# A weight stream through 51 pages: raw weights held by a table, or by the pages left free

## The chip, the cores and the metric

The kernel runs on one core of one Trainium2 chip. The core has a matrix engine (TensorE: PE in the profile, its weight loads PEld), a vector engine (VectorE: DVE), a scalar engine (ScalarE: ACT), a general engine (GpSimd: POOL) and a queue engine that issues transfers (SyncE: SP). Each takes its instructions in the order of the program and waits at semaphores for the others. The metric is the device time of one execution in microseconds (us); lower is better.

## The reference, cut to what matters

One layer of an encoder for 256 positions of width 2048, in float32: a gated feed-forward block, a mixer with two attention branches, a second feed-forward block, and an embedding gate; a layer norm follows each of the first three.

```
def _layer(x):                       # SEQ 256, D_MODEL 2048, D_FF 5632, DEPTH 1
    x = _layer_norm(ALPHA * x + 0.5 * _swiglu(x, ffn1_w1, ffn1_w3, ffn1_w2), ln1_g, ln1_b)
    mix = _hybrid_mixer(x, w_in, b_gates_m, conv_m, norm_m, w_up_m, w_up_sb, w_out)
    x = _layer_norm(ALPHA * x + mix, ln2_g, ln2_b)
    x = _layer_norm(ALPHA * x + 0.5 * _swiglu(x, ffn2_w1, ffn2_w3, ffn2_w2), ln3_g, ln3_b)
    return x + jax.nn.sigmoid(x @ w_ple_gate) * (p @ w_ple_proj)

def _swiglu(x, w1, w3, w2):
    return (jax.nn.silu(x @ w1) * (x @ w3)) @ w2

def _hybrid_mixer(...):
    mq, mk, mv, mo, mi, mf, sq, sk, sv, ga, gb = _split_cols(x @ w_in)
    ...                              # mLSTM heads -> y_m, stick-breaking heads -> y_sb
    merged = jax.nn.sigmoid(ga) * (y_m @ w_up_m) + jax.nn.sigmoid(gb) * (y_sb @ w_up_sb)
    return merged @ w_out
```

## The kernel before, in words

Nearly all the time goes into products of activations with weights that are read once from memory. A **raw** weight is a tile of 256 rows by 512 columns (512 KB). PE takes float32 as two halves of a narrower type (fp32r), so each weight is **split**: ACT casts the raw tile to the high half (line 1275), DVE subtracts that from the raw tile for the low half (line 1279). A **unit** is one weight times one block of 128 positions: six matmuls of 512 columns, three for each 128 rows: high by high (line 1331), high by low (1332), low by high (1333). The first matmul reads the high half of the weight and the second one the low half. The program has 1532 units and 1088 split weights.

Most weights are read by two units, one for each block of positions. In large parts of the feed-forward blocks and of the mixer a Strassen-like scheme (`seven`) stands in for eight products: it makes seven weights out of four raw tiles by adding raw tiles to each other, and each of them is read by one unit alone. Some of these sums are made by DVE (line 371, `plus`), some by a transfer that adds into the raw tile (line 377, `plus_load`, issued from POOL's queue right behind the subtraction of the weight before it, `soon`). `weave` puts the units of such a group between those of plain groups.

Raw tiles, split halves, and the activations all live in one pool of 51 **pages** of 4 KB per partition. A page that is given up goes to the next tile that is asked for; whoever writes that tile first waits until the last reader of the old one is done. A raw tile takes one page, a split weight two.

The order of all instructions is written out by a planner as the program is built. After every unit it lets due tasks run (evictions of results, transposes, the steps of the attention heads), then calls `splits_due` (line 1290), which splits weights while fewer than a limit are held; every split calls `loads`, which issues raw loads on SP's queue while fewer than a limit are held. Both limits come from `limits(j)` and the table

```
HELD = {"ffn": (11, 6), "mix": (6, 6), "woven": (9, 6), "wide": (11, 6)}
```

as (raw, split) for the stretch of the program that weight `j` is in; within six weights of a border between blocks they are 4 and 11. "ffn" holds for both feed-forward blocks, "woven" and then "wide" for the part of the mixer in which a second product is woven into the first, "mix" for the rest.

Of the kernel before, what the change touches and what calls it, by code (L numbers as in the profile page):

```python
# [24 lines left out]

PAGES = 51
TEMP_BUFS = 6


HELD = {"ffn": (11, 6), "mix": (6, 6), "woven": (9, 6), "wide": (11, 6)}  # L30
RAW_EDGE, SPLIT_EDGE = 4, 11
EDGE = 6

# [1 line left out]
PSUM_BUFS = 8  # L35
# [149 lines left out]
    return [p[0] for p in pairs] + [p[1] for p in pairs]  # L185


@with_exitstack
def kernel(
    ctx: ExitStack,  # L190
    tc: tile.TileContext,
    x, p, ffn1_w1, ffn1_w3, ffn1_w2, ln1_g, ln1_b, w_in, b_gates_m, conv_m, norm_m,
    w_up_m, w_up_sb, w_out, ln2_g, ln2_b, ffn2_w1, ffn2_w3, ffn2_w2, ln3_g, ln3_b,
    w_ple_gate, w_ple_proj, out,
):
    nc = tc.nc
    x, out = x[0], out[0]
    p = p[0, 0]
    w_in, w_out, w_up_m, w_up_sb = w_in[0], w_out[0], w_up_m[0], w_up_sb[0]

    consts = ctx.enter_context(tc.tile_pool(name="consts", bufs=1))
    dram_pool = ctx.enter_context(tc.tile_pool(name="dram", bufs=1, space=bass.MemoryType.DRAM))
    page_pool = ctx.enter_context(tc.tile_pool(name="page", bufs=PAGES))
    temp_pool = ctx.enter_context(tc.tile_pool(name="temp", bufs=TEMP_BUFS))
    small = ctx.enter_context(tc.tile_pool(name="small", bufs=4))
    ps_pool = ctx.enter_context(tc.tile_pool(name="ps", bufs=PSUM_BUFS, space=bass.MemoryType.PSUM))
    ctx.enter_context(tc.manual_schedule())

    sched = Sched()
    temps = [0]  # L210
# [49 lines left out]
    def load_x(c, t):  # L260
        nc.sync.dma_start(out=xres(t, c * COL), in_=x[t * P:(t + 1) * P, c * COL:(c + 1) * COL])
# [1004 lines left out]
    def split_one():  # L1266
        j = pos["split"]
        w = weights[j]
        make(j)
        assert w.made or not w.make  # L1270
        r = w.raw.tile[:, :, :w.cols]
        splits[j] = [page_pool.tile([P, 2, COL], F32R, name="split", tag="page") for _ in range(2)]
        hi, lo = (h[:, :, :w.cols] for h in splits[j])
        for ks in pieces(j):
            nc.scalar.copy(hi[:, ks], r[:, ks])  # L1275
# [3 lines left out]
            nc.vector.tensor_tensor(out=lo[:, ks], in0=r[:, ks], in1=hi[:, ks], op=ALU.subtract)  # L1279
        pos["split"] += 1  # L1280
        for f in w.soon:
            assert f.raw.tile is not None
            f.make()
            f.made = True
        pos["raw"] -= len(w.frees)
        for r in w.frees:
            r.tile = None
        loads()

    def splits_due():  # L1290
        most = pos["at"] + 3 if pos["at"] < 8 else len(weights)
        while pos["split"] < most and len(splits) < limits(pos["split"])[1]:
            split_one()
            if at_edge(pos["split"]):
                break

    for c in range(4):
        if c == 0:
            load_x(0, 0)
            loads(1)  # L1300
        for t in range(TT):
            if c:
                load_x(c, t)
            sched.spawn(start(c, t), max(0.01 * t, 5.2 * c + 1.3 * t - 2.6))
        loads(2 * c + 2)
    sched.run()
    split_one()
    sched.now = 0.02
    sched.run()
    splits_due()  # L1310
    warm(WARM2)
    make_tri()
    for u in program:
        if isinstance(u, (Boundary, Mode)):
            continue
# [12 lines left out]
        for k in range(2):  # L1328
            hi, lo = a[:, 0, u.sub + k], a[:, 1, u.sub + k]
            first, last = u.start and k == 0, u.stop and k == 1  # L1330
            nc.tensor.matmul(ps, hi, w[0][:, k, :u.cols], start=first, stop=False, skip_group_check=u.onto)  # L1331
            nc.tensor.matmul(ps, hi, w[1][:, k, :u.cols], start=False, stop=False, skip_group_check=u.onto)  # L1332
            nc.tensor.matmul(ps, lo, w[0][:, k, :u.cols], start=False, stop=last, skip_group_check=u.onto)  # L1333
# [35 lines left out]
```

## Time and profile before

| | |
|---|---|
| median of 3 runs | 2166.02 us (2165.04 to 2168.65) |
| the profiled execution | 2164.03 us |
| its span, first to last instruction | 2162.3 us |
| mean granted TensorE clock | 1.000 |
| instructions | 27685 |
| bytes moved | 535.98 MB, mean 248 GB/s |

The profile is of one execution. Its page gives, for each engine, the busy time and its share of the span; then the chain of work that ended last; then groups of equal instructions with count, total and mean; and, for each group, how long its engine stood idle just before it and what ended that. Matmuls are pipelined: one takes 0.39 us from start to end, but the next one starts after 0.23 us, so that busy times of matmuls overlap. Other views answer for one window of time, one source line or one engine's waits. Times within the execution are counted from the span's start.

### The profile page before, as it was taken

What the parts mean: (1) busy time and instruction counts of PE and PEld (TensorE: products, weight loads), DVE (VectorE), ACT (ScalarE), POOL (GpSimd) and SP (SyncE); (2) the same over time, 40 slices, a digit from 0 to 9 for tenths busy, and PEclk for the clock granted to TensorE, in tenths of its full rate; (3) what the DMA queues carried; (4) which work ended last, traced back from release to release, by engine and by line L of the source; (5) the groups of instructions that cost most, each with busy time, mean ns of one, the idle gap of its engine ahead of it and who ended that gap; (6) DMA issues with size and microseconds to landing.
All of it is one profiled execution on the core that took longest, in us unless ns stands there. A gap on an engine that the chain in (4) does not pass through costs nothing.

```text
span 2162.3 us, 27685 instructions
## 1 busy us (share of the span) xinstructions
PE 2153.1 (100%) x9798; PEld 1782.0 (82%) x9798; DVE 1897.6 (88%) x2096; ACT 1344.6 (62%) x1663; POOL 218.2 (10%) x186
## 2 busy tenths in 40 slices
PE   9999999999999999999999999999999999999999
PEld 7888888888888888888888888888888888888887
DVE  6899999999998898887888975799999999999974
ACT  7656656666665765677866563556656656666572
POOL 0111111111000000101011000011111111110000
PEclk9999999999999999999999999999999999999999
DMA  9899899999994667978898976579989999999642
GB/s 350 220 272 271 248 269 277 273 277 269 266 316 148 211 217 217 244 212 208 263 276 264 274 259 206 200 191 277 267 245 279 277 272 270 265 273 301 233 168 86
DMA packets 283179, 535.98 MB, mean 248 GB/s; under 512 B 17144, under 2 KB 34464, under 8 KB 283040
## 3 DMA queue, kind: packets, MB, share of 16 engines
q1 hardware_dynamic: 234624, 440.87, 60.0%
q0 software_dynamic: 48416, 93.33, 24.0%
q8 instruction: 77, 1.26, 0.2%
q14 instruction: 62, 0.51, 0.1%
HBM read 527.85 MB, written 6.29 MB: 247 GB/s over the span
## 4 chain that ended last, share of the span: by engine, by line
PE 91%; DVE 4%; issue 3%; DMA 2%; ACT 0%; POOL 0%; SPq 0%; DVEq 0%; POOLq 0%; ACTq 0%
PE mm L1331 29%; PE mm L1333 29%; PE mm L1332 29%; DMA raw<-in_ffn_w_dram 2%; DVE split L1279 2%; PE ms L298 1%; PE ms L524 0%; DVE actT L293 0%; POOL raw L377 0%; DVE raw L371 0%; PE ms L911 0%; PE ms L1019 0%; PE ms L989 0%; PE ms L926 0%; ACT split L1275 0%
## 5 line engine op out<-in xcount | busy, mean ns | idle before, releaser
L1275 ACT CAST split<-raw 128x1024 fp32r<-128x1024 f32 (+1 forms) x1089 | 1089.5, 1043 | 516.9 <-DMA raw<-in_ffn_w_dram 185.8
L1279 DVE TENSOR_TENSOR split<-raw,split 128x1024 fp32r<-128x1024 f32 (+1 forms) x1089 | 1277.1, 1210 | 136.6 <-ACT split L1275 128.5
L1331 PE MATMUL mm<-split,actT 128*128 128x512 f32 x3064 | 1201.2, 392 | 0.9 <-DVE actT L1025 0.9
L1333 PE MATMUL mm<-split,actT 128*128 128x512 f32 x3064 | 1187.7, 388 | 0.6 <-DVE actT L305 0.6
L1332 PE MATMUL mm<-split,actT 128*128 128x512 f32 x3064 | 1186.1, 387 | 0.4 <-DVE split L1279 0.4
L1333 PEld LDWEIGHTS mm<-split,actT 128*128 128x128 f32 x3064 | 575.1, 188 | 121.5 <-DVE actT L305 1.8
L1331 PEld LDWEIGHTS mm<-split,actT 128*128 128x128 f32 x3064 | 575.7, 188 | 115.5 <-ACT big L243 1.1
L1332 PEld LDWEIGHTS mm<-split,actT 128*128 128x128 f32 x3064 | 575.8, 188 | 114.5 <-DVE split L1279 1.7
L377 POOL DMA_DIRECT2D raw<-in_ffn_w_dram x140 | 169.7, 1440 | 1202.8 <-DVE split L1279 780.0
L371 DVE TENSOR_TENSOR raw<-raw 128x1024 f32<-128x1024 f32 x190 | 231.4, 1219 | 1.6
L377 POOL DMA_DIRECT2D raw<-in_w_in_dram x38 | 46.0, 1428 | 502.6 <-DVE split L1279 432.8
L300 ACT CAST actT<-ms 128x512 fp32r<-128x512 f32 x60 | 35.1, 586 | 73.6 <-PE ms L298 69.2
L649 DVE SCALAR_TENSOR_TENSOR big<-mm,big 128x512 f32<-128x512 f32 x112 | 76.3, 683 | 3.3 <-PE mm L1333 3.3
L597 DVE TENSOR_TENSOR temp<-mm,temp 128x512 f32<-128x512 f32 x108 | 73.1, 686 | 1.7 <-PE mm L1333 0.3
L305 DVE TENSOR_TENSOR actT<-ms,actT 128x512 fp32r<-128x512 f32 x60 | 40.9, 685 | 14.4 <-ACT big L304 9.3
L243 ACT ACTIVATE temp<-mm 128x512 f32<-128x512 f32 (+1 forms) x36 | 20.3, 569 | 49.9 <-PE mm L1333 49.9
L293 DVE TENSOR_TENSOR actT<-temp,actT 128x512 fp32r<-128x512 f32 x40 | 26.5, 687 | 17.3 <-ACT actT L292 17.2
L239 ACT ACT_TABLE_LOAD x30 | 38.5, 1283 | 0.5
L1191 DVE TENSOR_TENSOR temp<-temp,big 128x512 f32<-128x512 f32 (+1 forms) x10 | 5.8, 582 | 26.4 <-ACT temp L243 26.4
L292 ACT CAST actT<-temp 128x512 fp32r<-128x512 f32 x40 | 23.9, 620 | 8.0 <-DVE temp L316 7.4
L243 ACT ACTIVATE rstd<-mv,eps 128x1 f32<-128x1 f32 x6 | 1.8, 294 | 41.8 <-DVE mv L507 41.8
L1134 DVE SCALAR_TENSOR_TENSOR big<-big,mm 128x512 f32<-128x512 f32 x8 | 5.5, 686 | 25.3 <-PE mm L1333 25.3
(138 smaller groups left out, 613.1 us busy)
## 6 DMA issues: line engine op xcount, KB each, us to landing
raw<-in_ffn_w_dram SPq DMA_DIRECT2D x527, 512.0 KB, 7.0
raw<-in_w_in_dram SPq DMA_DIRECT2D x144, 512.0 KB, 5.1
raw<-in_ffn_w_dram POOLq DMA_DIRECT2D x140, 512.0 KB, 9.9
raw<-in_w_in_dram POOLq DMA_DIRECT2D x38, 512.0 KB, 8.4
raw<-in_w_out_dram SPq DMA_DIRECT2D x32, 512.0 KB, 5.3
raw<-in_w_ple_gate_dram SPq DMA_DIRECT2D x32, 512.0 KB, 5.0
raw<-in_w_in_dram SPq DMA_DIRECT2D x56, 256.0 KB, 4.1
raw<-in_w_up_m_dram SPq DMA_DIRECT2D x16, 512.0 KB, 6.3
```

The lines of the kernel that those rows point to most:

```text
L239: nc.scalar.preload_act_table_set(table[0])
L300: nc.scalar.copy(dst[:, 0], ps[:])
L305: nc.vector.tensor_tensor(out=dst[:, 1], in0=ps[:], in1=dst[:, 0], op=ALU.subtract)
L371: nc.vector.tensor_tensor(out=out.tile[:, :, :cols], in0=a.tile[:, :, :cols], in1=b.tile[:, :, :cols], op=ALU.add)
L377: nc.gpsimd.dma_start(out=out.tile[:, :, :cols], in_=src, accum_op=ALU.add)
L597: nc.vector.tensor_tensor(out=out, in0=a, in1=b, op=op)
L649: nc.vector.scalar_tensor_tensor(out=xs, in0=ps, scalar=0.5, in1=xs, op0=ALU.mult, op1=ALU.add)
L1275: nc.scalar.copy(hi[:, ks], r[:, ks])
L1279: nc.vector.tensor_tensor(out=lo[:, ks], in0=r[:, ks], in1=hi[:, ks], op=ALU.subtract)
L1331: nc.tensor.matmul(ps, hi, w[0][:, k, :u.cols], start=first, stop=False, skip_group_check=u.onto)
L1332: nc.tensor.matmul(ps, hi, w[1][:, k, :u.cols], start=False, stop=False, skip_group_check=u.onto)
L1333: nc.tensor.matmul(ps, lo, w[0][:, k, :u.cols], start=False, stop=last, skip_group_check=u.onto)
```

## The change

The raw limit is 16 in place of 11 or 9 in all stretches but "mix" (the entry "late" is used nowhere). To that comes a limit in pages. The program is first issued once to a stand-in for the core (`DryCore`) that records, for each page tile other than raw and split ones, the first and the last unit at which it is touched. From that `settle` works out `room`: at each unit the 51 pages less the most that those other tiles hold from the unit before it to the third one after it. In the real issue `full(more)` says whether the raw tiles held plus twice the split weights held plus `more` would go beyond that room. A load is held back by it once 5 raw tiles are held, a split always. The split that PE needs next is made in any case (`while pos["split"] <= j: split_one()` stands as it was).

```diff
-HELD = {"ffn": (11, 6), "mix": (6, 6), "woven": (9, 6), "wide": (11, 6)}
+HELD = {"ffn": (16, 6), "mix": (6, 6), "woven": (16, 6), "wide": (16, 6), "late": (16, 6)}
+AHEAD_UNITS = 4
...
+class Dry:                 # a stand-in tile: slices and views of it are itself
+class DryPool:             # gives stand-in tiles
+class DryCore:
+    def __call__(self, *args, **named):
+        for a in (*args, *named.values()):
+            if isinstance(a, Dry) and a.page is not None:
+                self.pages.touch(a.page)
...
+class Pages:
+    def touch(self, n):
+        first, _ = self.spans[n] or (self.unit, None)
+        self.spans[n] = first, self.unit
+    def tile(self, shape, dtype, name, tag):
+        if self.pool:
+            return self.pool.tile(shape, dtype, name=name, tag=tag)
+        if name in ("raw", "split"):
+            return Dry()
+        self.spans.append(None)
+        return Dry(len(self.spans) - 1)
+    def settle(self, pool):
+        used = [0] * (self.unit + 4)
+        for first, last in self.spans:
+            for u in range(first, last + 1):
+                used[u] += 1
+        self.room = [PAGES - max(used[max(u - 1, 0):u + AHEAD_UNITS]) for u in range(self.unit + 1)]
+        self.pool, self.unit = pool, 0
+    def left(self):
+        return self.room[self.unit] if self.room else PAGES
...
+    pages = Pages()
+    layer(DryCore(pages), pages, *[DryPool() for _ in range(5)], *args)
...
+    pages.settle(pool)
+    layer(tc.nc, pages, consts, dram_pool, temp_pool, small, ps_pool, *args)
...
+    def full(more):
+        return pos["raw"] + 2 * len(splits) + more > page_pool.left()
+
     def loads(most=len(raws)):
         while pos["load"] < most and pos["raw"] < (4 if pos["at"] < 6 else limits(pos["split"])[0]):
+            if pos["raw"] >= 5 and full(1):
+                break
...
-        while pos["split"] < most and len(splits) < limits(pos["split"])[1]:
+        while pos["split"] < most and len(splits) < limits(pos["split"])[1] and not full(2):
             split_one()
...
         sched.now += 6 * 0.2161 * u.cols / COL
+        page_pool.unit += 1
```

Both programs hold the same instructions in the same numbers; only their order and the pages differ. What the planner holds after some of the units, as raw tiles + split weights (the latter with the one that PE is at):

| after unit | 97 | 209 | 300 | 545 | 609 | 793 | 833 | 1020 | 1169 | 1353 |
|---|---|---|---|---|---|---|---|---|---|---|
| before | 11 + 6 | 11 + 6 | 11 + 6 | 6 + 6 | 9 + 6 | 11 + 6 | 11 + 6 | 11 + 6 | 11 + 6 | 11 + 6 |
| changed | 16 + 6 | 16 + 3 | 16 + 4 | 6 + 6 | 16 + 4 | 16 + 2 | 16 + 2 | 16 + 6 | 16 + 3 | 16 + 5 |

The pages tell when a split can be made. Call **distance** of a weight the number of units from the one whose end gives up the pages that its two halves take (the later of the two) to the unit that reads the weight first; a distance of 2 means that one unit lies between them. Counted in the two programs by the pages' addresses (the times are those at which the stretch runs before):

| units | us before | weights | distances before | distances in the changed program |
|---|---|---|---|---|
| 150 to 439, first feed-forward block | 219 to 620 | 231 | 5 or 6: 24, 7: 104, 8 and more: 103 | 3: 21, 4: 87, 5: 72, 6 and more: 51 |
| 600 to 699, mixer | 839 to 995 | 72 | 6: 2, 7: 9, 8 and more: 61 | 3: 8, 4: 19, 5: 31, 6 and more: 14 |
| 700 to 789, mixer | 995 to 1123 | 64 | 6: 18, 7: 23, 8 and more: 23 | 2: 5, 3: 24, 4: 21, 5 and more: 14 |
| 790 to 841, mixer | 1123 to 1195 | 38 | 4: 4, 5: 17, 6 and more: 17 | 1: 1, 2: 34, 3: 3 |
| 842 to 879, mixer | 1195 to 1247 | 27 | 6: 3, 7: 9, 8 and more: 15 | 3: 4, 4: 6, 5 and more: 17 |
| 1120 to 1399, second feed-forward block | 1585 to 1972 | 223 | 5 or 6: 24, 7: 104, 8 and more: 95 | 3: 21, 4: 87, 5: 70, 6 and more: 45 |

In the other stretches distances stay at 5 or more.

Two places, as rows of the built programs (the changed file's lines are higher by 72, from the new function `full` on by 77; the number behind a name is the buffer). The first is on ACT at units 798 to 804 of the mixer. `mm_9747` before and `mm_9740` in the changed program are the same result, of unit 799, which ACT takes out of PSUM with an activation. Before:

```order
L1275 CAST split_10022<-raw_9778 128x1024
L1275 CAST split_10035<-raw_9863 128x1024
L239 ACT_TABLE_LOAD
L243 ACTIVATE big_9660<-mm_9723 128x512
L1275 CAST split_10056<-raw_9697 128x1024
L243 ACTIVATE big_9689<-mm_9747 128x512
L1275 CAST split_10067<-raw_9912 128x1024
L1275 CAST split_10089<-raw_9935 128x1024
```

The changed program at the same place:

```order
L1352 CAST split_10043<-raw_9751 128x1024
L315 ACTIVATE big_9682<-mm_9740 128x512
L1352 CAST split_10056<-raw_9578 128x1024
L1352 CAST split_10075<-raw_9651 128x1024
L1095 CAST actT_9702<-ms_10089 128x128
L1095 CAST actT_9703<-ms_10089 128x128
L1352 CAST split_10096<-raw_9772 128x1024
```

Before, the cast right behind that eviction (`split_10067`) is read by PE from unit 807 on, eight units after unit 799; in the changed program the cast right behind it (`split_10056`) is read by unit 801, the next but one.

The second place is on DVE at units 278 to 284 of the first feed-forward block. `mm_3291` before and `mm_3288` in the changed program are both the result of unit 278. Before, from the eviction on:

```order
L649 SCALAR_TENSOR_TENSOR big_81<-mm_3291,big_81 128x512
L597 TENSOR_TENSOR temp_3195<-temp_3195,temp_3395 128x512
L635 SCALAR_TENSOR_TENSOR temp_3196<-temp_3196,temp_3066 128x512
L371 TENSOR_TENSOR raw_3203<-raw_3203,raw_3308 128x1024
L1279 TENSOR_TENSOR split_3473<-raw_3231,split_3472 128x1024
L1279 TENSOR_TENSOR split_3487<-raw_3203,split_3486 128x1024
L649 SCALAR_TENSOR_TENSOR big_83<-mm_3323,big_83 128x512
```

The changed program at the same place:

```order
L721 SCALAR_TENSOR_TENSOR big_81<-mm_3288,big_81 128x512
L669 TENSOR_TENSOR temp_3192<-temp_3192,temp_3392 128x512
L707 SCALAR_TENSOR_TENSOR temp_3193<-temp_3193,temp_3065 128x512
L1356 TENSOR_TENSOR split_3473<-raw_3228,split_3472 128x1024
L1356 TENSOR_TENSOR split_3486<-raw_3143,split_3485 128x1024
L721 SCALAR_TENSOR_TENSOR big_83<-mm_3321,big_83 128x512
L443 TENSOR_TENSOR raw_3143<-raw_3143,raw_3248 128x1024
```

The subtraction that follows the three evictions (`split_3473` in both) belongs to the weight that PE reads from unit 286 on before, and from unit 283 on in the changed program, so that the same burst of other DVE work stands three units nearer to PE.

More of the change, by code (lines that the diff above doesn't have):

```diff
@@ L185, in skewed, with __init__, __getitem__, _same @@
     return [p[0] for p in pairs] + [p[1] for p in pairs]
-@with_exitstack
-def kernel(
-    ctx: ExitStack,
-    tc: tile.TileContext,
+class Dry:
+    def __init__(self, page=None):
+        self.page = page
+    def __getitem__(self, _):
+        return self
+    def _same(self, *_, **__):
+        return self
+    rearrange = bitcast = broadcast_to = _same
+class DryPool:
+    def tile(self, *_, **__):
+        return Dry()
+class DryCore:
+    def __init__(self, pages):
+        self.pages = pages
+    def __getattr__(self, _):
+        return self
+    def __call__(self, *args, **named):
+        for a in (*args, *named.values()):
+            if isinstance(a, Dry) and a.page is not None:
+                self.pages.touch(a.page)
@@ new lines, with __init__ @@
+class Pages:
+    def __init__(self):
+        self.pool, self.unit, self.spans, self.room = None, 0, [], None
+    def touch(self, n):
[5 more added lines that the diff above has]
+        if name in ("raw", "split"):
+            return Dry()
+        self.spans.append(None)
[9 more added lines that the diff above has]
+        return self.room[self.unit] if self.room else PAGES
@@ new lines, with kernel @@
+@with_exitstack
+def kernel(ctx: ExitStack, tc: tile.TileContext, *args):
+    pages = Pages()
+    layer(DryCore(pages), pages, *[DryPool() for _ in range(5)], *args)
+    pool = ctx.enter_context(tc.tile_pool(name="page", bufs=PAGES))
+    consts = ctx.enter_context(tc.tile_pool(name="consts", bufs=1))
+    dram_pool = ctx.enter_context(tc.tile_pool(name="dram", bufs=1, space=bass.MemoryType.DRAM))
+    temp_pool = ctx.enter_context(tc.tile_pool(name="temp", bufs=TEMP_BUFS))
+    small = ctx.enter_context(tc.tile_pool(name="small", bufs=4))
+    ps_pool = ctx.enter_context(tc.tile_pool(name="ps", bufs=PSUM_BUFS, space=bass.MemoryType.PSUM))
+    ctx.enter_context(tc.manual_schedule())
+    pages.settle(pool)
+    layer(tc.nc, pages, consts, dram_pool, temp_pool, small, ps_pool, *args)
@@ L192, with layer @@
+def layer(
+    nc, page_pool, consts, dram_pool, temp_pool, small, ps_pool,
     x, p, ffn1_w1, ffn1_w3, ffn1_w2, ln1_g, ln1_b, w_in, b_gates_m, conv_m, norm_m,
@@ L195 @@
 ):
-    nc = tc.nc
     x, out = x[0], out[0]
@@ L199 @@
     w_in, w_out, w_up_m, w_up_sb = w_in[0], w_out[0], w_up_m[0], w_up_sb[0]
[L201 to L207, printed above, removed]
     sched = Sched()
```

## The prediction, made before the changed kernel had run

> **What bounds the kernel now.** I read the page first, then PE's waits, then who waits for the loads, then the stretches in which the program's order changes. The page's first part and the shares of the chain:
>
> ```profile
> PE 2153.1 (100%) x9798; PEld 1782.0 (82%) x9798; DVE 1897.6 (88%) x2096; ACT 1344.6 (62%) x1663; POOL 218.2 (10%) x186
> ...
> PE 91%; DVE 4%; issue 3%; DMA 2%; ACT 0%; POOL 0%; SPq 0%; DVEq 0%; POOLq 0%; ACTq 0%
> ```
>
> PE is busy all the time and makes up nearly the whole chain; DVE is next. A busy PE could still wait inside, so here are all its waits:
>
> ```profile
> PE ms L1209 <- DVE ones L247: 1.1, 1, 1.1
> PE mm L1331 <- DVE actT L1025: 0.9, 1, 0.9
> PE ms L298 <- DMA big<-in_x_dram: 0.7, 1, 0.7
> PE mm L1333 <- DVE actT L305: 0.6, 2, 0.3
> PE mm L1332 <- DVE split L1279: 0.4, 1, 0.4
> PE ms L298 <- DVE actT L305: 0.4, 1, 0.4
> ```
>
> That is 4.1 us in the whole execution. Whatever comes earlier by this change, no more than these can come back, and of them only 0.4 us is a wait for a weight. The time can hardly fall; the question is how much it rises. Next, a unit's pace, from the rows of PE by time:
>
> ```profile
> 352.36 0.39 PE L1331 MATMUL mm<-split,actT 128*128 128x512 f32 x1
> 352.58 0.39 PE L1332 MATMUL mm<-split,actT 128*128 128x512 f32 x1
> ...
> 353.72 0.39 PE L1331 MATMUL mm<-split,actT 128*128 128x512 f32 x1
> ```
>
> The rows left out are four more matmuls: a unit takes 1.36 us, and it wants the low half of its weight 0.22 us after its start.
>
> **Who waits for a raw load, and who for a page.** The change holds more raw tiles. Who waits for the raw loads of line 1249 (first fence), for the adding transfers of line 377 (second), and what the casts wait for in all (third):
>
> ```profile
> POOL raw L377: 134.7, 5
> ACT split L1275: 7.1, 6
> DVE split L1279: 2.5, 2
> ```
>
> ```profile
> ACT split L1275: 185.1, 94
> ```
>
> ```profile
> ACT split L1275 <- DMA raw<-in_ffn_w_dram: 185.8, 95, 4.0
> ACT split L1275 <- PE mm L1332: 76.5, 63, 4.2
> ACT split L1275 <- PE mm L1333: 52.9, 62, 3.4
> ```
>
> The casts wait 185.8 us for transfers, but 185.1 us of that is for the adding ones, which start only when an earlier split is done; a raw tile that comes sooner does not start them. For the raw loads proper the casts wait 7.1 us. Another 129.4 us they wait for PE, that is for pages. So the change gives pages to tiles that were hardly waited for, and takes them from splits that do wait for pages.
>
> **What a page wait is worth.** A cast that waited for its page, and its subtraction, in the mixer:
>
> ```profile
> 1156.67 1.06 ACT L1275 CAST split<-raw 128x1024 fp32r<-128x1024 f32 x1 [2.07 <-PE mm L1332]
> 1157.76 1.22 DVE L1279 TENSOR_TENSOR split<-raw,split 128x1024 fp32r<-128x1024 f32 x1
> ```
>
> ```profile
> 1156.70 0.39 PE L1331 MATMUL mm<-split,actT 128*128 128x512 f32 x1
> ```
>
> The cast starts as the unit ends that gave up the page (PE's next one starts at 1156.70), and the low half is there at 1158.98: 2.31 us from page to weight, with nothing in between. At distance d there are d-1 units and 0.22 us for it. That leaves 0.73 us too little at d = 2, and to spare 0.63 us at d = 3, 1.99 at 4, 3.35 at 5 and 6.07 at 7. Before, nearly all distances are 5 or more; now many are 2 to 4.
>
> What eats the spare time is other work of ACT and DVE between page and weight, so here are the stretches that the table of distances names, by engine (PE, PEld, DVE, ACT, POOL busy; clock; DMA share; GB/s):
>
> ```profile
> 219.00:620.00 401.00, 401.00 (x1797) 331.98 (x1796) 376.31 (x370) 247.99 (x264) 58.17 (x48) 1.00 0.95 270
> 995.00:1123.00 128.00, 127.06 (x637) 107.57 (x636) 106.22 (x145) 100.77 (x168) 14.53 (x12) 1.00 0.85 241
> 1123.00:1195.00 72.00, 72.00 (x321) 59.71 (x320) 61.99 (x62) 46.16 (x51) 7.28 (x6) 1.00 0.90 266
> ```
>
> and what of it is splitting, first for 995 to 1123 us, then for 1123 to 1195 us:
>
> ```profile
> L1279 DVE TENSOR_TENSOR split<-raw,split 128x1024 fp32r<-128x1024 f32 (+1 forms) x64 | 72.8, 1154 | 18.3 <-ACT split L1275 17.5 <-PE mm L1332 0.7
> ...
> L1275 ACT CAST split<-raw 128x1024 fp32r<-128x1024 f32 (+1 forms) x63 | 61.6, 997 | 13.6 <-PE mm L1332 4.8 <-PE mm L1333 3.3 <-PE ms L989 1.6
> ```
>
> ```profile
> L1279 DVE TENSOR_TENSOR split<-raw,split 128x1024 fp32r<-128x1024 f32 x39 | 47.2, 1222 | 10.4 <-ACT split L1275 7.8 <-PE mm L1332 2.0
> ...
> L1275 ACT CAST split<-raw 128x1024 fp32r<-128x1024 f32 x39 | 40.5, 1052 | 26.5 <-PE mm L1332 14.4 <-PE mm L1333 8.0 <-DVE split L1279 3.2
> ```
>
> **The change part by part.** The first issue to the stand-in emits nothing, and both programs have the same instructions, so no work is added or removed on any engine.
>
> *Term 1, units 790 to 841.* 34 of 38 weights come to d = 2. One round is two units: page, cast, subtraction, unit. Of 52 units that is 26 rounds, each 0.73 us too long: 19 us. Other work there is 46.2 - 40.5 = 5.7 us on ACT and 62.0 - 47.2 = 14.8 us on DVE, 20.5 us; the first place shown above has such work, an eviction, right ahead of a cast that is due two units later. If all of it falls beside PE's unit it costs nothing, if all falls into the round, 20.5 us. I take half, since the evictions follow units and the sums by DVE are made ahead: 29 us, ends 19 and 40.
>
> *Term 2, units 700 to 789.* Other work is 100.8 - 61.6 = 39.2 us on ACT and 106.2 - 72.8 = 33.4 us on DVE, 0.81 us per unit. The 24 weights at d = 3 stand for 24/64 of 90 units, 11 rounds of three units; half of the 2.4 us of other work in a round goes beyond the 0.63 us to spare by 0.57 us: 6 us. The five at d = 2 cost 0.73 us and half of 1.6 us each: 8 us. At d = 4 half of the other work (1.6 us) just fits; 2 us for bursts. Together 16 us; 4 if other work costs nothing, 45 if it all counts.
>
> *Term 3, both feed-forward blocks.* 108 of 231 and 108 of 223 weights come to d = 3 or 4. Here other work comes in bursts. One of them, on DVE by time (the place of the second pair of rows above):
>
> ```profile
> 399.67 0.68 DVE L649 SCALAR_TENSOR_TENSOR big<-mm,big 128x512 f32<-128x512 f32 x1
> 400.27 0.68 DVE L597 TENSOR_TENSOR temp<-temp 128x512 f32<-128x512 f32 x1
> 400.87 0.69 DVE L635 SCALAR_TENSOR_TENSOR temp<-temp 128x512 f32<-128x512 f32 x1
> 401.47 1.22 DVE L371 TENSOR_TENSOR raw<-raw 128x1024 f32<-128x1024 f32 x1
> 402.61 2.48 DVE L1279 TENSOR_TENSOR split<-raw,split 128x1024 fp32r<-128x1024 f32 x2
> ```
>
> Four instructions stand in front of the subtraction for 402.61 - 399.67 = 2.94 us. At d = 7 the spare 6.07 us cover that; at d = 4 it is 0.95 us too much, about 1 us of PE's time. A group of seven products takes about 65 us (401 us for some six) and has two such bursts: 12 per block, 12 us per block, 24 us together. Ends: 0, if DVE runs ahead enough; 35 per block if casts late by a page make DVE the bound, which has 401.0 - 376.3 = 24.7 us left there and would be short of it if each of 231 weights made it wait some 0.26 us.
>
> *Term 4, units 600 to 699 and 842 to 879.* 12 weights at d = 3, at term 2's 0.57 us: 7 us; ends 0 and 20.
>
> *At nothing:* the five more loads at the first rise of the limit (unit 14) stand behind those needed first on SP's queue. On SP the loads stand some eight units further ahead of their use, so what is queued behind them (norm rows, results put away) is asked for at the same place and waits for no page later than before. POOL's adding transfers still follow their subtraction.
>
> Sum: 29 + 16 + 24 + 7 = 76 us on the profiled execution's 2164.0 us: 2240; the median of the runs stands 2.0 us above it, so 2242 us. Low ends: 23 us, 2189; high ends: 40 + 45 + 70 + 20 = 175 us, 2341.
>
> **The rivals.** *Two weights in hand suffice.* While PE works on one weight ACT and DVE make the next, and a round of page, cast and subtraction hides behind the unit in between. Then term 1 and the 8 us at d = 2 fall away: 2242 - 37 = 2205 us. Against it stand 2.31 us against 1.58. It decides if casts turn out to start before the unit's end. [...]
>
> *The adding transfers come late as well.* They start at a subtraction; where it comes later against PE, so does the landing, and 94 casts wait for landings already. At 1 us of PE for each: 2242 + 94 = 2336 us. Against it, a wait for a page and one for a landing in the same round are not paid twice.
>
> *Nothing to be measured.* ACT and DVE, 62% and 88% busy, make up for every late page: within 0.2%, 2162 to 2170 us (0.2%, about 4 us, is what a measurement of this kernel can tell from no change).
>
> *Faster.* The deeper loads end POOL's 134.7 us and the casts' 7.1 us, and the adding transfers start sooner. At best that returns PE's 4.1 us: 2162 us. It needs every split at d = 2 in time, since 26 late rounds of 0.16 us would already undo it.
>
> **How the numbers follow.** The forecast's mechanism, between 2210 and 2290 us, gets 0.58; two weights in hand, 2171 to 2210 us, 0.16; the adding transfers or DVE as the bound, above 2290 us, 0.16; nothing to be measured 0.07; faster 0.03. The range leaves out the last two, the mildest of the second and the worst of the third: 2190 to 2325 us.
>
> **What would show it.** PE's waits for `split L1279` rise from 0.4 us to some 60 us or more, the largest share between 1120 and 1200 us, where units then go 1.5 to 2 us apart instead of 1.36; ACT's waits for PE rise far above 129.4 us; ACT's 185.8 us for transfers stay near that, as no raw load was in them. Each late low half shows as a gap between a unit's first and second matmul. The start (to unit 150) and the end (from unit 1400) keep their time. The forecast is wrong if stretch 1123 to 1195 us keeps its 72 us, or if the feed-forward blocks lose more than the mixer.

## The result, and the profile after

The changed kernel takes 2221.52 us (median of 4 runs, 2219.95 to 2224.46) against 2165.53 us for the kernel before on the same chip: a ratio of 1.0257, 95% interval 1.0239 to 1.0275. It is slower by 56 us. The forecast was 2242 us with a range of 2190 to 2325.

The page of the changed kernel, its span and its busy engines:

```profile
span 2219.9 us, 27812 instructions
...
PE 2174.6 (98%) x9798; PEld 1777.5 (80%) x9798; DVE 1906.6 (86%) x2096; ACT 1362.7 (61%) x1663; POOL 218.3 (10%) x186
```

The engines do the same work in the same number of instructions; the 127 more than before (27812 against 27685) are all semaphore instructions, mainly of ACT and DVE, so "the same instructions in the same numbers" above holds for the work alone. The span has grown by 57.6 us. PE's own waits, in us, times and the longest:

```profile
PE mm L1409 <- DVE split L1356: 31.8, 44, 2.2
PE ms L1091 <- DVE temp L1082: 1.9, 1, 1.9
PE mm L1408 <- ACT split L1352: 1.7, 4, 0.8
```

What PE waits for is now the low half of a weight: 31.8 us in 44 waits, where it was 0.4 us in one. And what the casts wait for, from all waits:

```profile
ACT split L1352 <- PE mm L1409: 151.7, 153, 4.2
...
ACT split L1352 <- DVE raw L443: 113.0, 64, 4.6
ACT split L1352 <- DMA raw<-in_ffn_w_dram: 104.8, 54, 4.0
ACT split L1352 <- PE mm L1410: 89.8, 104, 3.5
```

The casts' waits for PE rise from 129.4 to 241.5 us (151.7 + 89.8), and those for transfers fall from 185.8 to 104.8 us. That fits casts that wait longer for their pages and find their data landed meanwhile.

The stretches of the forecast's terms, in the columns used before (us; busy PE, PEld, DVE, ACT, POOL; clock; DMA share; GB/s): the first feed-forward block, units 700 to 789, units 790 to 841, the second feed-forward block.

```profile
218.70:632.60 413.90, 406.54 (x1797) 330.27 (x1796) 380.67 (x371) 254.27 (x265) 58.18 (x48) 1.00 0.93 263
1009.30:1148.50 139.20, 130.06 (x635) 106.68 (x635) 105.12 (x143) 100.17 (x167) 12.11 (x10) 1.00 0.80 227
1148.50:1239.90 91.40, 79.60 (x321) 59.06 (x320) 63.48 (x62) 46.32 (x51) 9.70 (x8) 0.98 0.74 209
1629.50:2028.10 398.60, 391.78 (x1733) 318.75 (x1732) 368.55 (x360) 244.68 (x253) 58.20 (x48) 1.00 0.93 263
```

Cut at the start of the first matmul of the same unit in both executions, the rise lies here:

| units | us before | us after | rise | forecast |
|---|---|---|---|---|
| 0 to 149 | 211.7 | 211.4 | -0.3 | 0 |
| 150 to 439, feed-forward | 401.1 | 413.9 | 12.8 | 12 |
| 440 to 599 | 219.3 | 219.8 | 0.5 | 0 |
| 600 to 699, mixer | 155.8 | 156.8 | 1.0 | 7, with 842 to 879 |
| 700 to 789, mixer | 127.6 | 139.2 | 11.6 | 16 |
| 790 to 841, mixer | 72.0 | 91.4 | 19.4 | 29 |
| 842 to 1119 | 390.2 | 389.5 | -0.7 | see 600 to 699 |
| 1120 to 1399, feed-forward | 387.0 | 398.7 | 11.7 | 12 |
| 1400 to end | 190.3 | 191.8 | 1.5 | 0 |

So the rise lies where it was forecast to lie, but for the fourth term's 7 us. Whether it has the cause that was given is another question, and the experiments are about that.

### The profile page after: what moved, and what is told of

Its sections match the earlier page's. It is cut to its first block, busy times and chain, and to the rows that moved or that the text cites. A ratio compares the mean times of both kernels' runs of the same rounds, so it can differ in the third digit from the quotient of the medians.

```text
span 2219.9 us, 27812 instructions
## 1 busy us (share of the span) xinstructions
PE 2174.6 (98%) x9798; PEld 1777.5 (80%) x9798; DVE 1906.6 (86%) x2096; ACT 1362.7 (61%) x1663; POOL 218.3 (10%) x186
## 5 line engine op out<-in xcount | busy, mean ns | idle before, releaser
L1352 ACT CAST split<-raw 128x1024 fp32r<-128x1024 f32 (+1 forms) x1089 | 1104.3, 1044 | 529.0 <-PE mm L1409 151.7
L1409 PE MATMUL mm<-split,actT 128*128 128x512 f32 x3064 | 1195.1, 390 | 32.8 <-DVE split L1356 31.8
L315 ACT ACTIVATE temp<-ms,gbT 128x128 f32<-128x128 f32 x64 | 24.1, 460 | 5.6 <-PE ms L596 5.6
```

The costliest lines, as they stand in the source:

```text
L315: nc.scalar.activation(out, in_, func, **kw)
```

## The experiments

Eleven kernels were run. The edits are against the changed kernel unless said otherwise. "Rise by stretch" is against the same units of the kernel before, in the order: units 790 to 841, units 700 to 789, first feed-forward block, second one. The changed kernel has 19.4, 11.6, 12.8, 11.7.

| kernel | us | ratio to before (95%) | rise by stretch |
|---|---|---|---|
| splits_first | 2170.58 | 1.0026 (1.0016 to 1.0036) | 0.0, 0.0, 0.7, 2.2 |
| raw_as_before | 2163.20 | 0.9989 (0.9980 to 0.9998) | 0.0, -1.2, -0.1, -0.1 |
| spare_pages | 2207.07 | 1.0190 (1.0173 to 1.0207) | 13.4, 6.9, 11.1, 10.2 |
| halves | 2211.48 | 1.0213 (1.0198 to 1.0229) | 8.3, 12.1, 12.7, 12.1 |
| three_ahead | 2312.08 | 1.0683 (1.0667 to 1.0699) | 3.5, 10.7, 27.3, 31.8 |
| two_ahead | 2643.76 | 1.2217 (1.2199 to 1.2236) | 13.0, 52.6, 95.5, 90.3 |
| spare_first | 2180.77 | 1.0074 (1.0059 to 1.0089) | 3.8, 0.5, 4.3, 4.9 |
| after_first | 2216.21 | 1.0235 (1.0218 to 1.0252) | 12.2, 13.4, 12.4, 11.4 |
| before_first | 2182.17 | 1.0078 (1.0061 to 1.0095) | 0.3, 1.9, 3.9, 4.3 |
| raw13 | 2167.10 | 1.0009 (0.9999 to 1.0018) | 1.7, -0.7, 1.7, 0.6 |
| raw15 | 2187.96 | 1.0106 (1.0090 to 1.0122) | 6.4, 2.5, 6.7, 5.4 |

### splits_first: six weights split at a time, raw tiles in what pages are left

```diff
-            if pos["raw"] >= 5 and full(1):
+            if pos["raw"] >= 5 and pos["raw"] + 2 * limits(pos["split"])[1] + 1 > page_pool.left():
...
-        while pos["split"] < most and len(splits) < limits(pos["split"])[1] and not full(2):
+        while pos["split"] < most and len(splits) < limits(pos["split"])[1]:
```

> The raw limit stays 16 and the room in pages stays, but a split is no longer held back by it; instead a load is held back so that six split weights always find room. The planner then holds 6 splits and 9 to 16 raw tiles (9 in units 790 to 841, 13 to 15 in the feed-forward blocks), and all distances are 5 or more. Theory P (a split waits for a page that PE has not yet given up): the whole rise goes, 2162 to 2170 us, and units 790 to 841 take 72 us again. Theory L (more loads in flight make transfers land later, the adding ones above all): the feed-forward blocks still hold 13 to 15 raw tiles in place of 11 and keep about half or more of their 24 us, 2175 to 2190 us.

Measured: 2170.58 us. The whole rise of the four stretches is gone but for 2.8 us, with 8 to 16 raw tiles held and six split weights nearly throughout. So where the loads are deeper than before (11 to 16 raw tiles in the feed-forward blocks) they are not what costs, and they bring nothing either, since PE had next to nothing to wait for. In units 790 to 841 only 8 or 9 are held nearly throughout, fewer than the 11 before, so of deep loads there this kernel says nothing. PE's waits for low halves are nearly gone, but the casts' waits for PE are as long here as in the changed kernel:

```profile
PE mm L1409 <- DVE split L1356: 2.9, 3, 1.2
...
ACT split L1352 <- PE mm L1409: 157.1, 144, 4.2
...
ACT split L1352 <- PE mm L1410: 90.4, 120, 3.4
```

The casts wait 247.5 us, against 241.5 us there, and PE does not mind: a cast that waits for a page six units ahead of its use has time. That a cast waits for PE does not by itself say that PE will wait for it.

### raw_as_before: the rule by pages with the old table

```diff
-HELD = {"ffn": (16, 6), "mix": (6, 6), "woven": (16, 6), "wide": (16, 6), "late": (16, 6)}
+HELD = {"ffn": (11, 6), "mix": (6, 6), "woven": (9, 6), "wide": (11, 6)}
```

> The rule by pages stays, with the old table's raw limits (11, 9 and 11 in place of 16). In units 700 to 841 the rule still holds splits back, to 5 and for some units 4, distances 4 to 6 there; elsewhere nothing changes against the kernel before. Theory P: at distance 4 there are 2 us to spare, so 2164 to 2170 us, with at most 3 us in units 700 to 841. A rival, that the rule itself (splits made by room and not by count) disturbs the order: some of the 19 us in units 790 to 841 stays, 2172 us or more.

Measured: 2163.20 us, 2 us below the kernel before: the interval just leaves out 1 (0.9980 to 0.9998), but the difference is 0.1%. The first issue to a stand-in and the rule by pages cost nothing; the numbers 16 do.

### spare_pages: as few split weights as the changed kernel, but pages free

The old raw limits, and a rule that stops splits at the same numbers as the changed kernel has after each unit, so that 5 to 7 pages stay empty:

```diff
-HELD = {"ffn": (16, 6), "mix": (6, 6), "woven": (16, 6), "wide": (16, 6), "late": (16, 6)}
+HELD = {"ffn": (11, 6), "mix": (6, 6), "woven": (9, 6), "wide": (11, 6)}
...
-        while ... and not full(2):
+        while ... and not full(2 + max(16 - limits(pos["split"])[0], 0) * (limits(pos["split"])[0] in (9, 11))):
```

> Raw limits as before (11, 9, 11), but splits held back as if there were 16: the planner holds the same numbers of split weights after every unit as the changed kernel (2 in units 790 to 841, 4 or 5 in the feed-forward blocks) while five or seven pages lie empty, so that distances are 4 to 7 again. Theory P: pages are free long before they are needed, so most of the rise goes, 2165 to 2180 us, though casts stand behind more evictions. Theory Q (it is the place of the split in the engines' order, fewer weights ahead, that costs): the rise stays, 2210 to 2225 us. Theory L: all of it goes, 2166 us.

Measured: 2207.07 us. Distances are back at 4 and more (one weight has 3), yet three quarters of the rise stay (42 of 56 us). The wait for the page was taken away, as the casts' waits for PE show (62.9 us, where the changed kernel has 241.5), and PE still waits for 33 low halves:

```profile
ACT split L1352 <- DVE raw L443: 229.9, 105, 5.0
...
ACT split L1352 <- PE mm L1409: 36.9, 24, 4.2
ACT split L1352 <- PE mm L1410: 26.0, 18, 3.4
...
PE mm L1409 <- DVE split L1356: 23.3, 33, 2.2
```

What took the page's place is seen in PE's longest wait, which is the same in both kernels to the hundredth. First the changed kernel, rows by time (start and duration in us; in brackets the idle time before, and what ended it):

```profile
1174.84 1.05 ACT L1352 CAST split<-raw 128x1024 fp32r<-128x1024 f32 x1 [0.35 <-DVE split L1356]
...
1177.68 1.42 DVE L497 TENSOR_TENSOR big<-mm,big 128x512 f32<-128x512 f32 x2 [1.75 <-PE mm L1410]
...
1178.84 0.39 PE L1408 MATMUL mm<-split,actT 128*128 128x512 f32 x1
1179.02 1.22 DVE L443 TENSOR_TENSOR raw<-raw 128x1024 f32<-128x1024 f32 x1
1180.15 1.22 DVE L1356 TENSOR_TENSOR split<-raw,split 128x1024 fp32r<-128x1024 f32 x1
...
1181.42 0.50 PE L1409 MATMUL mm<-split,actT 128*128 128x512 f32 x1 [2.19 <-DVE split L1356]
...
1181.76 0.40 PE L1410 MATMUL mm<-split,actT 128*128 128x512 f32 x1
```

Then the kernel with pages free, the same units:

```profile
1164.93 3.90 ACT L1352 CAST split<-raw 128x1024 fp32r<-128x1024 f32 x4
...
1170.17 1.42 DVE L497 TENSOR_TENSOR big<-mm,big 128x512 f32<-128x512 f32 x2 [1.79 <-PE mm L1410]
...
1171.33 0.39 PE L1408 MATMUL mm<-split,actT 128*128 128x512 f32 x1
1171.51 1.21 DVE L443 TENSOR_TENSOR raw<-raw 128x1024 f32<-128x1024 f32 x1
1172.64 1.22 DVE L1356 TENSOR_TENSOR split<-raw,split 128x1024 fp32r<-128x1024 f32 x1
...
1173.91 0.50 PE L1409 MATMUL mm<-split,actT 128*128 128x512 f32 x1 [2.19 <-DVE split L1356]
```

The cast of the weight in question was done long before in both, by 1175.89 in the first and by 1168.83 at the latest in the second; it had its page. What is late is its subtraction. DVE stands idle for 1.75 and 1.79 us until a unit ends, since the evictions of line 497 read that unit's result; it takes that out in 1.42 us, makes a sum of raw tiles for a weight to come (1.2 us, put between cast and subtraction by `split_one`), and then the subtraction (1.22 us), while PE, which has begun the weight's unit already, waits for 2.19 us. Since the same order of instructions does it in both, there are two mechanisms that hold a split to the end of a unit close ahead of its use: the wait for a page (the forecast's), and the place in the order of DVE and ACT behind evictions. The second follows from how few weights are held split: with six, the same subtraction would have been issued some units earlier, and that of a later weight would stand behind these evictions.

### halves: the same splits in two pieces, units 790 to 841

```diff
-        for ks in pieces(j):
+        for ks in pieces(0 if 569 <= j <= 606 else j):
```

Weights 569 to 606 are split as two halves of 128 rows each, so that PE's second matmul waits for a cast and a subtraction of half the size.

> The changed kernel, with the splits of the 38 weights of units 790 to 841 made in two halves of 128 rows each, so that PE can start on the first half while the second is made. Distances are the same as in the changed kernel. Theory P: the time from page to what PE needs first falls from 2.31 us to some 1.3 us (a cast of 0.6 us and a subtraction of 0.7 us for half the columns, an estimate from the 512-wide ones), less than the 1.58 us at distance 2, so these units fall from 91.4 us to 72 to 78 us and the whole to 2202 to 2210 us; all other stretches keep their times. Theory L: no change, 2221 us.

Measured: in the stretch concerned the rise falls from 19.4 to 8.3 us, less far than expected; the others keep theirs within 0.5 us. Of the fall, 1.7 us are a phase at half clock that the changed kernel has in this stretch and this one has not (see the last section). The length of the chain from cast to low half is thus on PE's path there, but halving it does not remove the loss; that the evictions and sums ahead of a subtraction stay as long as they were fits that.

### three_ahead and two_ahead: fewer weights split, in the kernel before

These two are edits of the kernel before, with pages free in plenty:

```diff
-HELD = {"ffn": (11, 6), "mix": (6, 6), "woven": (9, 6), "wide": (11, 6)}
+HELD = {"ffn": (11, 3), "mix": (6, 3), "woven": (9, 3), "wide": (11, 3)}
```

and with 2 in place of 3.

> The kernel before with one number changed: 3 weights split at a time in place of 6, raw tiles as before. Pages are then free in plenty: those that a split takes were last used 4 units or more ahead, as in the kernel before, so nearly no split waits for one. Theory Q (what counts is how many weights stand split ahead in the order in which ACT and DVE work; a split that is issued only two or three units ahead of its use stands behind evictions that wait for PE): units 700 to 789 lose about the 6.9 us that they lost with the same number and pages free, units 790 to 841, which had 2 there and lost 13.4, lose about 5, each feed-forward block, which had 4 to 5 and lost 11, loses 15 to 25; together 2200 to 2225 us. Theory P (the wait for the page is the cost): within 5 us of the kernel before, 2165 to 2170 us.

> As the kernel with 3 weights split at a time, with 2: the weight in use and one ahead, pages last used 4 units or more ahead for nearly all. Theory Q: units 790 to 841 lose the 13.4 us that they lost with 2 and pages free, units 700 to 789 twice their 6.9, each feed-forward block 30 or more, and the stretches that kept their time so far (units 14 to 150, 880 to 1120) lose too; together 2260 us or more. Theory P: 2165 to 2170 us. A rule that two buffers suffice: 2165 to 2170 us as well.

PE's waits with three and with two:

```profile
PE mm L1332 <- DVE split L1279: 73.9, 67, 3.3
```

```profile
PE mm L1332 <- DVE split L1279: 248.3, 290, 3.0
PE mm L1331 <- ACT split L1275: 47.6, 89, 2.1
```

Measured: 2312 us with three (expected 2200 to 2225), 2644 us with two (expected 2260 or more). The page alone, or a rule by which two buffers suffice, gave 2165 to 2170 us for both, and is out by 142 us and more. The number held costs time with pages free. Units 790 to 841 lose 13.0 us with two, as they lost 13.4 us with two and pages free in the kernel above: the same number, the same loss. The size was underrated for three, partly since the expectation left out the stretches in which the changed kernel holds six (among others, units 440 to 599 lose 20.3 us, 14 to 149 11.9 us, 1400 to the end 13.6 us), partly since the feed-forward blocks lose 27.3 and 31.8 us, above the 15 to 25 expected; three weights in hand do not cover their bursts on DVE.

### spare_first, after_first, before_first: splits ahead of the evictions

If the place behind evictions is what makes a split late, issuing the splits that become due at a unit ahead of that unit's evictions must help. The same edit in three kernels: that with few weights split and pages free, the changed one, and the kernel before.

```diff
         if u.tile.uses == 0:
             splits.pop(j)
+        splits_due()
         if u.stop:
             u.done(ps, u.tt)
```

> The kernel that splits as few weights ahead as the changed one but keeps 5 to 7 pages empty (2207.07 us), with the splits that become due at a unit issued ahead of that unit's evictions and other work, not behind them. Number of splits and pages as there. If a split is late because it stands behind evictions that wait for PE, units 790 to 841 fall from +13.4 to +5 us or less and each feed-forward block from +11 to +6 or less: 2180 to 2192 us. If only the number counts, or the amount of ACT's and DVE's work, the time stays at 2203 to 2211 us.

> The changed kernel with the splits that become due at a unit issued ahead of that unit's evictions, not behind them; raw tiles, splits held and pages as in the changed kernel, so a split still takes the page that this unit gives up and waits for its end. If standing behind evictions is most of the loss: 2195 to 2207 us, of units 790 to 841 the 19.4 us fall to about 10. If the wait for the page is: 2217 to 2225 us, as the page comes free at the same time. If evictions that stand behind a cast now come late for PE: above 2225 us.

> The kernel before with the splits that become due at a unit issued ahead of that unit's evictions. With 6 weights held split and pages free it should not matter in which order they stand: 2163 to 2168 us. If the evictions behind the casts come late for PE: 2172 us or more, with PE's waits for evicted tiles risen.

Measured: 2180.77, 2216.21 and 2182.17 us. With the plain order beside it:

| splits stand | six split, pages free | few split, pages free | few split, pages tight |
|---|---|---|---|
| behind the evictions | 2165 (before) | 2207 (spare_pages) | 2222 (changed) |
| ahead of them | 2182 (before_first) | 2181 (spare_first) | 2216 (after_first) |

The first is what was expected if the place behind evictions makes a split late. The second lies between what was expected from the evictions (2195 to 2207 us) and from the page (2217 to 2225 us), close to the latter. The third was a miss: with six weights split the order should not have mattered, and it costs 17 us (2182 against 2165). Other work now comes late for PE; its longest waits are those of its transposes (line 298) for what DVE takes out of earlier ones (line 305), and of a few products inside the attention heads:

```profile
PE ms L298 <- DVE actT L305: 10.6, 8, 3.0
PE ms L807 <- ACT temp L795: 2.7, 1, 2.7
PE ms L1008 <- DVE actT L1004: 2.2, 1, 2.2
```

So each row has to be read against its own first column. In the lower row, where the place in the order is not in question, few split weights cost nothing in all with pages free (2181 against 2182), and 34 us with pages tight. That is the page's wait by itself, and it is real. The nothing is a balance: units 790 to 841 rise by 3.8 us with few weights and by 0.3 us with six, while units 0 to 149 rise by 1.2 and 5.2 us, so that in the stretch with two weights in hand some cost is left that neither the page nor the evictions account for; its cause stays open. With pages free, PE's waits for low halves go from 23.3 us behind the evictions (shown under `spare_pages`) to the first of these lines ahead of them. The second line has splits first and pages tight:

```profile
PE mm L1409 <- DVE split L1356: 5.4, 11, 0.8
```

```profile
PE mm L1409 <- DVE split L1356: 23.3, 35, 1.6
```

In the upper row few weights cost 42 us with pages free, which is the place in the order by itself, and tight pages add only 14 us to that, since a split that is held to the end of a unit by one of the two loses little more by the other. Taking away one alone gives back 14 us (the page) or 5 us (the place, at the price of the evictions), and both together 41 us.

By stretch the pages weigh differently. Units 700 to 789 lose 0.5 us with splits first and pages free, and 13.4 us with splits first and pages tight, of which 3.4 us are two phases at half clock: the page alone suffices for the loss there. Units 790 to 841 go from 3.8 to 12.2 us, the feed-forward blocks from 4.3 and 4.9 to 12.4 and 11.4 us, where 0.3 us, and 3.9 and 4.3 us, are the price of the order itself. The casts' waits in the changed kernel with splits first, and in the one with pages free:

```profile
ACT split L1352 <- PE mm L1409: 181.9, 185, 4.2
...
ACT split L1352 <- PE mm L1410: 112.2, 140, 3.8
```

```profile
ACT split L1352 <- PE mm L1410: 52.0, 34, 5.7
ACT split L1352 <- PE mm L1409: 42.0, 37, 5.1
```

294.1 us of waits for PE in the first, 94.0 us in the second. One reservation: the two kernels differ in the raw tiles held as well (16 against 11); that these by themselves cost little is known from splits_first for the feed-forward blocks, but not for units 790 to 841.

### raw13 and raw15: how the loss grows

```diff
-HELD = {"ffn": (16, 6), "mix": (6, 6), "woven": (16, 6), "wide": (16, 6), "late": (16, 6)}
+HELD = {"ffn": (13, 6), "mix": (6, 6), "woven": (13, 6), "wide": (13, 6), "late": (13, 6)}
```

and with 15 in place of 13.

> The changed kernel with at most 13 raw tiles in place of 16, the rule by free pages kept. 5 or 6 weights are then held split in the feed-forward blocks, 4 or 5 in units 700 to 789 and mostly 4 in units 790 to 841, of pages last used 3 to 7 units ahead. If a split is late only where it is held to the end of a unit close ahead of its use, whether by its page or by the evictions ahead of it: units 790 to 841 lose 0 to 3 us, each feed-forward block 0 to 1, together 2163 to 2172 us. If deep loads cost something of their own (transfers that collide): above 2175 us.

> As the kernel with at most 13 raw tiles, with 15: mostly 5 weights held split in the feed-forward blocks (4 to 5 at 16), 3 or 4 in units 700 to 789, 3 in units 790 to 841 (2 at 16), of pages last used 3 units ahead or more for nearly all. If the loss follows the number held: units 790 to 841 lose 5 to 10 us, units 700 to 789 4 to 8, each feed-forward block 3 to 8; 2182 to 2200 us. If it goes in proportion to the raw tiles added: four fifths of the rise, about 2210 us.

PE's waits for low halves with 13 and with 15:

```profile
PE mm L1409 <- DVE split L1356: 1.7, 4, 0.6
```

```profile
PE mm L1409 <- DVE split L1356: 13.5, 22, 1.3
```

Measured: 2167.10 and 2187.96 us, both within what was expected by the number held; of the stretches, units 700 to 789 lose less than expected with 15 (2.5 us for 4 to 8) and the first feed-forward block more with 13 (1.7 us for 0 to 1). With 11 raw tiles at most, 13, 15 and 16 the rule by pages costs -2, 2, 23 and 56 us: the loss is not in proportion to the raw tiles but sets in where they leave fewer than about four weights split in units 790 to 841 (mostly 5, 4, 3 and 2 there, which lose 0.0, 1.7, 6.4 and 19.4 us).

## Why the prediction was right, and where it was not

The sign, the time and the place were right: 2242 forecast, 2221.5 measured, and the stretches of the first three terms lost time while those outside the terms kept theirs within 1.5 us. The stretches of the fourth term kept theirs too, against the forecast.

*What bounds the kernel, and what could come back.* Right. PE was full, no more than its 4.1 us could come back, and neither the deeper loads (splits_first) nor anything else tried gave more than 2 us.

*What a page wait is worth.* Half right. The chain of 2.31 us from page to weight against 1.58 us, so 0.73 us too little at a distance of 2, shows in units 790 to 841 as it was worked out: 18 gaps of more than 0.13 us between a unit's first and second matmul, of 0.71 us in the median. One of them, by time in the changed kernel:

```profile
1187.36 1.23 DVE L1356 TENSOR_TENSOR split<-raw,split 128x1024 fp32r<-128x1024 f32 x1 [0.67 <-ACT split L1352]
1188.62 1.06 ACT L1352 CAST split<-raw 128x1024 fp32r<-128x1024 f32 x1 [1.98 <-DVE split L1356]
1189.71 1.22 DVE L1356 TENSOR_TENSOR split<-raw,split 128x1024 fp32r<-128x1024 f32 x1 [1.12 <-ACT split L1352]
...
1190.99 0.50 PE L1409 MATMUL mm<-split,actT 128*128 128x512 f32 x1 [0.55 <-DVE split L1356]
```

The page that this cast waits for was given up by the subtraction before it, which read its raw tile from there, so that ACT and DVE work by turns in place of side by side. In this stretch such waits are longer than those for PE:

```profile
ACT split L1352 <- DVE split L1356: 21.5, 15, 2.5
ACT split L1352 <- PE mm L1409: 14.1, 9, 2.9
```

The forecast had counted pages given up by PE alone. And with splits ahead of the evictions the wait for pages costs 34 us by itself. But the step took it that a late split waits for its page, so that there is no loss without that wait; with pages free and the order as it is, 42 of the 56 us stay. The other work of ACT and DVE, which the step let "eat the spare time" behind a page, holds the split to the end of a unit on its own, because evictions wait for that unit in front of it. The loss has two causes that lie over each other, and the forecast named one.

*Term 1, units 790 to 841: 29 us forecast, 19.4 measured,* at the low end of 19 to 40. Not 26 rounds but 18 came late, 14.9 us in all between first and second matmul. So 26 x 0.73 us was too many rounds of the right size, and of the other work, put at 10 us, less was paid than that, in single long waits as the one of 2.19 us.

*Term 2, units 700 to 789: 16 us forecast, 11.6 measured.* 9 gaps, 6.5 us in all; the 24 weights at a distance of 3 were mostly in time. Not in the forecast were two waits of products in the attention heads for what DVE wrote, 1.9 us (line 1091, shown with the result) and 1.3 us (line 1080).

*Term 3, both feed-forward blocks: 24 us forecast, 24.5 measured.* The count was nearly right, 12 bursts per block, where 13 gaps are seen in each, 9.5 and 8.9 us in all. The bursts were the mechanism, with the page as the smaller part: with pages free 11.1 and 10.2 us stay, so that standing behind the burst is what counts, as the fence with four instructions ahead of the subtraction had it.

*Term 4, units 600 to 699 and 842 to 879: 7 us forecast, 1.0 measured.* Distances of 3 cost next to nothing there, so that the 0.57 us taken over from term 2 was the wrong size.

*What would show it.* The casts' waits for PE rose (129.4 to 241.5 us), but splits_first, which has 247.5 us of them and loses 5 us, shows that this sign proves little. PE's waits for the low half came to 31.8 us, not 60 or more. Part of the difference is the restart: the matmul after a wait starts 0.34 us ahead of the next one in place of 0.23, and the wait counts only from the end of the matmul before, 0.39 us after its start in place of 0.23. At 0.11 + 0.16 = 0.27 us for each of 44 waits that is an estimate of 12 us. Units in 790 to 841 go 1.76 us apart (91.4 us for 52), within the 1.5 to 2 forecast. That the casts' waits for transfers stay near 185.8 us was wrong: 104.8 us. The adding transfers start at a subtraction, but it seems that the casts that wait for them are now held back by other things first, so that less of the wait is left for the landing.

*The rivals.* Two weights in hand do not suffice: units 790 to 841 lose 13.0 us with two and pages free, and the whole kernel 479 us with two throughout. The Trainium skill ("Trainium Kernel Development and Optimization", Best Practices: "Double-buffer for performance") gives its advice for overlapping DMA with compute. Carried over to weights that ACT and DVE prepare, of which the page does not speak, it would have left both at their time, and the measurement decides against that. Of adding transfers that come late there is no sign: the casts' waits for landings fell. Nothing to be measured, and faster, did not occur.

## What to carry to other kernels

Where engines work in the order of the program, a tile that is prepared ahead needs two distances, one from the end of the work that frees its memory and one from the instructions ahead of it in its engines' queues that wait for that same work; a shortage in either is enough, and repairing one alone can look as if it were not the cause. A memory limit shared by two stages should first hold the number of tiles of the later stage (here six split weights, and no fewer than four) and give the earlier stage what is left: splits_first lost 5 us where the opposite order lost 56. And before a buffer is deepened, look up who waits for it: the raw loads were waited for 7.1 us by casts that were not late.

## What the runs showed of the hardware beside that

After PE's wait of 2.19 us, shown above, the granted clock went down by itself. In windows of the changed kernel (us; busy PE, PEld, DVE, ACT, POOL; clock; DMA share; GB/s):

```profile
1178.50:1181.42 2.92, 0.73 (x4) 0.27 (x3) 2.92 (x4) 1.05 (x1) 0.00 (x0) 1.00 0.58 180
1181.50:1183.00 1.50, 1.50 (x6) 1.16 (x6) 1.47 (x3) 0.19 (x1) 0.00 (x0) 0.77 0.38 64
1183.00:1185.70 2.70, 2.45 (x6) 1.49 (x5) 2.70 (x4) 0.96 (x2) 0.00 (x0) 0.50 0.65 222
1185.70:1190.00 4.30, 4.30 (x20) 3.55 (x19) 2.51 (x3) 2.32 (x3) 0.00 (x0) 1.00 0.48 170
```

About 1 us after PE has resumed the clock goes down to half, and from 1185.70 us it is full again: some 3.4 us at half speed, which is an estimate of 1.7 us lost on top of the 2.19. The kernel with pages free shows the same behind the same wait (clock 0.98 in units 790 to 841). Of the 43 other times above 0.3 us in which PE stands idle in the changed kernel from the first unit on, all of them shorter (1.90 us at most), none has such a phase behind it. It is not certain, though. Over all thirteen profiled executions, full clock ended during the wait or within 3.5 us after it in 40 of 49 waits of 2 us or more, in 11 of 37 between 1.5 and 2 us, and in 3 of 81 between 1 and 1.5 us; one of 2.69 us with two weights split had no such phase. Where waits are many it adds up; with two weights split at a time:

```profile
core 0: 2647.4 us, clock 0.977
```

A clock short by 0.023 over 2647.4 us is an estimate of 61 us, of the 479 that this kernel lost.

The Trainium skill ("TensorE: Matmul & The Clock Gate", Part 1 on the clock gate) puts the drop behind at least one idle window of about 3.4 us. Here 2.19 us of waiting were enough, and most waits of 2 us or more were, so that a weight that is very late mostly costs more than its lateness.
